# One-hot rows of the chosen keys compared for eight tokens in one instruction instead of four

## The chip, the cores and the metric

The kernel runs on one core of one Trainium2 chip. The time is the device time of one execution in microseconds (us), the median of three runs. A core has a matrix engine (TensorE, PE in the profile; PEld is its loading of weights), a vector engine (VectorE, DVE), an activation engine (ScalarE, ACT), a general engine (GpSimd, POOL) and a queue that issues transfers (SyncE, SP). Each engine runs its own instructions in the order in which they stand in the program; between engines they wait on semaphores.

## The reference, cut to what matters

The kernel computes two transformer blocks for 512 tokens of width 1024. The change lies in the expert layer of the first block. For each token, 8 heads choose 16 pairs of keys (e1, e2) out of 128 by 128, which name 128 of 16,384 experts, each with a gate; the output is a gated sum over these experts.

```
e1 = jnp.take_along_axis(i1, ic // PEER_TOPK, axis=-1)
e2 = jnp.take_along_axis(i2, ic % PEER_TOPK, axis=-1)
idx = (e1 * N_KEYS + e2).reshape(T, PEER_HEADS * PEER_TOPK)
gate = jax.nn.softmax(vc, axis=-1).reshape(T, PEER_HEADS * PEER_TOPK)
...
u = expert_u[ib]
pre = jnp.einsum('td,tkd->tk', xb, u).astype(jnp.float32)
a = jax.nn.gelu(pre, approximate=False) * gb
return jnp.einsum('tk,tkd->td', a, expert_v[ib])
```

## The kernel before

For 384 of the 512 tokens the kernel multiplies every token with every expert and weighs the products with a dense table of gates, G[e1, e2, token], which is zero where an expert was not chosen. (The last 128 tokens are done by gathering rows, later.) The table is made in what is called the gate stage here: 96 steps of four tokens each, a software pipeline of four parts, whose loop variable is `q`.

- `g_hot` (line 957): DVE compares, for four tokens, the chosen keys with a constant `iota4` (0 to 127, each value four times). The keys lie in `eT`, one chosen pair per partition, token along the free dimension. The result `eb` is of shape [128, 2, 128, 4] in bf16: for half 0 (e1) and half 1 (e2), for each of the 128 key values, for each of the four tokens, a 1 where the key was chosen. The token is the innermost run. There are two buffers of `eb`.
- `g_wide` (line 967): `eb` is read with key and token exchanged, so that a token's 128 values lie in a row. ACT copies half 1 to `o2` in float32 (line 970). For `o1`, half 0 is multiplied with the gates `gT` (line 972); that is done by GpSimd in 60 of the steps and by DVE in 36 of them. Both have three buffers.
- `g_sum` (line 975): PE makes, for each of the four tokens, the 128 by 128 product of `o2` and `o1` into `gps`. In the profile a product in float32 is two records. Behind each step it issues one or two matmuls of `early_products` (line 814, `acc<-XT,wraw`), which compute ahead some of the products of the next stage; they need neither `eb` nor `o1`.
- `g_out` (line 981): ACT copies `gps` to a staging buffer (`gst` or `rows`), which is sent to memory every eight steps from the queue of GpSimd (line 992).

Two more things run in this stage. `pair_keys` (line 911) makes the keys of the next 128 tokens, one piece every five steps: DVE compares and adds (lines 918 to 949), and one multiplication `eq<-eq,ib` of 2048 elements is done by GpSimd (line 933). And GpSimd's queue issues the transfer of each finished early product (line 824), for which it waits in its order.

The tile framework's scheduler sets the order of the instructions on each engine, from the order in which they are written and from its own estimates; behind the stage comes the loop over the experts (`prepare`, `u_product`, `v_product`), whose matmuls with line 1100 and 206 to 208 make up most of the time. `cload` (line 159) loads a constant through GpSimd's queue.

Of the kernel before, what the change touches and what calls it, by code (L numbers as in the profile page):

```python
# [12 lines left out]
BF16 = mybir.dt.bfloat16  # L13
U32 = mybir.dt.uint32
AF = mybir.ActivationFunctionType
OP = mybir.AluOpType
# [13 lines left out]
def t5_bucket(d):  # L30
    n, mx = 32, 2048
    e = n // 2
    nf = np.maximum(d, 1).astype(np.float32)
    large = e + (np.log(nf / np.float32(e)) / np.log(mx / e) * (n - e)).astype(np.int32)
    large = np.minimum(large, n - 1)
    return np.where(d < e, d, large)


def na_layout():

    def tile_(kind, n):
        r = np.repeat(np.arange(8), 16)
        if kind == "b":
            return r, n * 16 + np.tile(np.arange(16), 8)
        r8, w = np.repeat(np.arange(8), 8), np.tile(np.arange(8), 8)
        return np.concatenate([r8, r8]), np.concatenate([n * 16 + 8 + w, (n + 2) * 16 + w])

    seq = [tile_("b", 0), tile_("b", 1), tile_("m", 0), tile_("m", 1), tile_("b", 2), tile_("b", 3)]  # L50
    qr, qw = np.repeat(np.arange(8), 16), np.tile(np.arange(16), 8)
    dr = np.zeros((128, 4, 256), int)
    dc = np.zeros((128, 4, 256), int)
    ok = np.zeros((128, 4, 256), bool)
    for cb, first in enumerate(NA_FIRST):
        kr = np.concatenate([seq[first][0], seq[first + 1][0]])[None]
        kc = np.concatenate([seq[first][1], seq[first + 1][1]])[None]
        qc = cb * 16 + qw[:, None]
        lo = np.clip(qc - 8, 0, 48)
        dr[:, cb] = kr - qr[:, None] + 7  # L60
        dc[:, cb] = np.clip(kc - qc, -15, 15) + 15
        ok[:, cb] = (kc >= lo) & (kc < lo + 16)
    return dr, dc, np.where(ok, 0, NEG).astype(np.float32)


def const_arrays():
    f = np.float32
    c = {}

    sel4 = np.zeros((4, 4, 128), f)  # L70
    col4 = np.zeros((128, 4, 4), f)
    for h in range(4):
        sel4[h, h] = 1
        col4[:, h, h] = 1
    c["sel4"] = sel4
    c["col4"] = col4
    j, i = np.arange(128)[:, None], np.arange(128)[None, :]
    c["cmaskT"] = np.where(j <= i, 0, NEG).astype(f)

    d = 511 - np.arange(640)  # L80
    oh = np.zeros((32, 640), f)
    ok = d >= 0
    oh[t5_bucket(np.maximum(d, 0))[ok], np.nonzero(ok)[0]] = 1
    c["t5oh"] = oh
    cnt = (d <= 128).astype(int) + (d % 4 == 0) + (d % 16 == 0)
    cnt = np.where(ok, cnt, 0)
    ln = np.where(cnt > 0, np.log(np.maximum(cnt, 1)), NEG).astype(f)
    c["t5ln"] = np.broadcast_to(ln, (8, 640)).copy()
    c["na_mask"] = na_layout()[2]
    i, k = np.arange(128)[:, None], np.arange(384)[None]  # L90
    m = np.where(np.abs(i - (k - 128)) <= 128, 0, NEG).astype(f)
    z = np.zeros((128, 256), f)
    c["swa_mask"] = np.concatenate([z, m, z], 1)

    t = np.arange(T)
    inv = np.power(f(10000.0), -np.arange(16, dtype=f) / f(16)).astype(f)
    ang = np.concatenate([(t // 64).astype(f)[:, None] * inv, (t % 64).astype(f)[:, None] * inv], 1)
    cos, sin = np.cos(ang).astype(f), np.sin(ang).astype(f)
    tab = np.stack([np.concatenate([cos, cos], 1), np.concatenate([-sin, sin], 1)], 1)
    c["rope"] = np.ascontiguousarray(tab.reshape(4, 128, 2, 64).transpose(1, 0, 2, 3))  # L100

    c["iota4"] = np.broadcast_to(np.repeat(np.arange(128), 4).astype(f), (128, 512)).copy()
    c["rank16"] = np.broadcast_to(np.repeat(np.arange(16), 128).astype(f), (128, 2048)).copy()
    return c

# [2 lines left out]
def body(ctx: ExitStack, tc: tile.TileContext, a: dict, out: bass.AP, dbg=None, stop=None):  # L108
# [8 lines left out]
    ve, se, pe, gp, sy = nc.vector, nc.scalar, nc.tensor, nc.gpsimd, nc.sync  # L117

    def pool(stack, name, bufs=1, **kw):
        return stack.enter_context(tc.tile_pool(name=name, bufs=bufs, **kw))  # L120
# [17 lines left out]
    def t2(n=T, name="t2", p=128):  # L138
        return tp.tile([p, n], F32, name=name, tag="t2")
# [19 lines left out]
    def cload(pl, name, shape, dt=F32):  # L159
        t = pl.tile(shape, dt, name=name)  # L160
        gp.dma_start(t, a[name])
        return t
# [261 lines left out]
    with ExitStack() as mx:  # L424
# [172 lines left out]
        for hd in range(4):  # L597
# [25 lines left out]
            q = t2(T, "E")  # L623
# [145 lines left out]
    with ExitStack() as ex:  # L769
# [20 lines left out]
        eT = kp.tile([128, 2, T], BF16, name="eT")  # L790
# [43 lines left out]
        with ExitStack() as gx:  # L834
# [15 lines left out]
            for hd in range(8):  # L850
                for half in range(2):
# [7 lines left out]
                    q = t2(name="pq")  # L859
# [45 lines left out]
        with ExitStack() as gx:  # L905
            gk = pool(gx, "ghot")
            gst_ = [rows[:, :4].rearrange("p r n -> p (r n)"),
                    pool(gx, "gstage").tile([128, NE * TG], F32, name="gst")]
            iota4 = cload(gk, "iota4", [128, 512], BF16)
            i4 = iota4.rearrange("p (e t) -> p e t", t=4)  # L910
            def pair_keys(t, eng):

                tps = mix([128, 2, 128], "ktp") if t != TS else None
# [41 lines left out]


            def g_hot(it):
                tok = it["tok"]
                it["eb"] = eb = gk.tile([128, 2, 128, 4], BF16, name="eb", bufs=2)
                ve.tensor_tensor(eb, i4.unsqueeze(1).to_broadcast([128, 2, 128, 4]),  # L960
                                 eT[:, :, tok].unsqueeze(2).to_broadcast([128, 2, 128, 4]), OP.is_equal)

                t, q = divmod(it["q"], 32)
                if t < TS and q % 5 == 3:
                    next(keys[t + 1], None)
# [32 lines left out]
            for _ in keys[0]:  # L998
                ahead(10)
            pipeline([dict(q=th * (TG // 4) + tg, th=th, tg=tg, tok=slice(th * TG + tg * 4, th * TG + tg * 4 + 4))  # L1000
                      for th in range(ND // TG) for tg in range(TG // 4)], g_hot, g_wide, g_sum, g_out)
        pp.close()
        b1.close()
# [715 lines left out]
def layout(i):  # L1719
    f = np.float32  # L1720
    o = dict(const_arrays())
    o["xT"] = np.ascontiguousarray(i["x"][0].T)
    w = i["w_in"][0]
# [74 lines left out]
```

## Time and profile before

| what | us |
|---|---|
| median of three runs (range) | 3405.89 (3403.52 to 3408.29) |
| the profiled execution, its own time | 3405.12 |
| its span, first to last instruction | 3403.4 |
| PE busy | 3278.4 (96%) |
| DVE busy | 2352.6 (69%) |
| ACT busy | 1239.5 (36%) |
| POOL busy | 680.9 (20%) |
| the gate stage | about 585 to 776 of the span |

Busy time is the time in which an engine has an instruction under way, also while that instruction is held up. PE is busy nearly all the time over the whole span; the gate stage, some 191 us, is a small part of it and has limits of its own.

### The profile page before, as it was taken

What the parts mean: (1) busy time and instruction counts of PE and PEld (TensorE: products, weight loads), DVE (VectorE), ACT (ScalarE), POOL (GpSimd) and SP (SyncE); (2) the same over time, 40 slices, a digit from 0 to 9 for tenths busy, and PEclk for the clock granted to TensorE, in tenths of its full rate; (3) what the DMA queues carried; (4) which work ended last, traced back from release to release, by engine and by line L of the source; (5) the groups of instructions that cost most, each with busy time, mean ns of one, the idle gap of its engine ahead of it and who ended that gap; (6) DMA issues with size and microseconds to landing.
All of it is one profiled execution on the core that took longest, in us unless ns stands there. A gap on an engine that the chain in (4) does not pass through costs nothing.

```text
span 3403.4 us, 49823 instructions
## 1 busy us (share of the span) xinstructions
PE 3278.4 (96%) x19091; PEld 2762.9 (81%) x19091; DVE 2352.6 (69%) x4718; ACT 1239.5 (36%) x2138; POOL 680.9 (20%) x695
## 2 busy tenths in 40 slices
PE   7889999898999999999999999999999998989999
PEld 5565766677999999999989887888888887878887
DVE  5345678875777777777765557587767778757776
ACT  4134211563333333333354546321221236632221
POOL 0000011564444444444311222000000001100000
PEclk9989999999999999999999999999999999999999
DMA  4535564459888888888832212221111211023331
GB/s 155 196 116 173 176 211 145 165 194 343 296 317 310 307 300 317 305 305 312 287 114 77 72 64 72 68 83 64 67 62 62 62 39 32 14 76 117 94 99 56
DMA packets 151990, 538.07 MB, mean 158 GB/s; under 512 B 17988, under 2 KB 23332, under 8 KB 150216
## 3 DMA queue, kind: packets, MB, share of 16 engines
q1 hardware_dynamic: 97920, 326.76, 28.4%
q0 software_dynamic: 52800, 205.51, 16.9%
q8 instruction: 150, 2.46, 0.3%
q10 hardware_dynamic: 1032, 2.62, 0.2%
q14 instruction: 88, 0.72, 0.1%
HBM read 497.24 MB, written 40.13 MB: 158 GB/s over the span
## 4 chain that ended last, share of the span: by engine, by line
PE 85%; DVE 6%; DMA 3%; issue 2%; ACT 2%; POOL 1%; SPq 0%; POOLq 0%; DVEq 0%; ACTq 0%
PE pv L1100 15%; PE acc L206 11%; PE acc L207 11%; PE acc L208 11%; PE acc L232 9%; PE pd L200 3%; PE pd L199 3%; PE pd L201 3%; PE pt L347 2%; PE acc L814 2%; DMA mraw<-in_w_mod_dram 2%; PE gps L978 1%; PE mod L392 1%; PE on L1400 1%; DVE eb L960 1%
## 5 line engine op out<-in xcount | busy, mean ns | idle before, releaser
L206 PE MATMUL acc<-hh,wh 128*128 128x512 f32 (+1 forms) x1728 | 638.0, 370 | 4.9 <-DVE cg L1205 2.3
L207 PE MATMUL acc<-hl,wh 128*128 128x512 f32 (+1 forms) x1728 | 633.1, 366 | 0.0
L208 PE MATMUL acc<-hh,wl 128*128 128x512 f32 (+1 forms) x1728 | 632.2, 366 | 0.0
L206 PEld LDWEIGHTS acc<-hh,wh 128*128 128x128 f32 x1728 | 326.1, 189 | 51.4 <-issue 8.1
L207 PEld LDWEIGHTS acc<-hl,wh 128*128 128x128 f32 x1728 | 326.1, 189 | 39.4 <-issue 1.2
L208 PEld LDWEIGHTS acc<-hh,wl 128*128 128x128 f32 x1728 | 325.7, 188 | 39.3 <-issue 2.2
L183 ACT ACTIVATE wh<-wraw 128x1024 fp32r<-128x1024 f32 (+1 forms) x189 | 198.9, 1054 | 393.9 <-PE acc L207 168.0
L1100 PE MATMUL pv<-vl,ah 128*128 128x512 f32 x768 | 302.3, 394 | 10.5 <-DVE vl L1080 10.5
L1100 PE MATMUL pv<-vh,al 128*128 128x512 f32 x768 | 302.4, 394 | 0.0
L184 DVE TENSOR_TENSOR wl<-wraw,wh 128x1024 fp32r<-128x1024 f32 (+1 forms) x189 | 230.7, 1222 | 102.3 <-ACT wh L183 98.9
L1100 PE MATMUL pv<-vh,ah 128*128 128x512 f32 x768 | 298.2, 389 | 0.0
L1016 POOL DMA_INDIRECT rows<-in_expert_v_dram,sidx x128 | 191.1, 1493 | 231.5 <-DVE tok L1031 204.6
L1016 POOL DMA_INDIRECT rows<-in_expert_u_rows_dram,sidx x128 | 180.0, 1406 | 229.3 <-DVE rows L1021 217.7
L232 PE MATMUL acc<-wh,hh 128*128 128x256 f32 (+1 forms) x624 | 195.6, 314 | 3.9 <-ACT hh L183 2.3
L232 PE MATMUL acc<-wh,hl 128*128 128x256 f32 (+1 forms) x624 | 193.3, 310 | 0.0
L232 PE MATMUL acc<-wl,hh 128*128 128x256 f32 (+1 forms) x624 | 192.9, 309 | 0.0
L1074 DVE TENSOR_TENSOR al<-ge,ah 128x384 fp32r<-128x384 f32 x128 | 71.3, 557 | 171.7 <-ACT ah L1072 171.2
L1072 ACT ACTIVATE ah<-ge 128x384 fp32r<-128x384 f32 x128 | 67.3, 526 | 328.7 <-PE pv L1100 286.2
L1100 PEld LDWEIGHTS pv<-vl,ah 128*128 128x128 f32 x768 | 144.9, 189 | 39.2 <-DVE vl L1080 10.8
L1100 PEld LDWEIGHTS pv<-vh,al 128*128 128x128 f32 x768 | 145.0, 189 | 30.4
L1021 DVE SCALAR_TENSOR_TENSOR rows<-rows,tok 128x1024 f32<-128x1024 f32 x128 | 154.5, 1218 | 20.1 <-issue 17.4
L1100 PEld LDWEIGHTS pv<-vh,ah 128*128 128x128 f32 x768 | 144.5, 188 | 27.8
(460 smaller groups left out, 7349.4 us busy)
## 6 DMA issues: line engine op xcount, KB each, us to landing
wraw<-in_expert_u_dram SPq DMA_DIRECT2D x128, 512.0 KB, 5.8
vraw<-in_expert_v_dram SPq DMA_DIRECT2D x127, 512.0 KB, 4.8
mraw<-in_w_mod_dram SPq DMA_DIRECT2D x96, 512.0 KB, 4.2
wraw<-in_ffn_up_dram SPq DMA_DIRECT2D x88, 512.0 KB, 3.5
gt<-gdr POOLq DMA_DIRECT2D x31, 768.0 KB, 9.1
wraw<-in_ffn_down_dram SPq DMA_DIRECT2D x44, 512.0 KB, 4.0
gdr<-gst POOLq DMA_DIRECT2D x6, 2048.0 KB, 7.7
gdr<-rows POOLq DMA_DIRECT2D x6, 2048.0 KB, 7.6
```

Source lines behind the costliest of these rows:

```text
L183: se.activation(hi, src, AF.Copy)
L184: ve.tensor_tensor(lo, src, hi.bitcast(F32), OP.subtract)
L199: pe.matmul(ps, wh[i], xh[i], start=i == 0, stop=False)
L200: pe.matmul(ps, wh[i], xl[i], start=False, stop=False)
L201: pe.matmul(ps, wl[i], xh[i], start=False, stop=i == n - 1)
L206: pe.matmul(ps, wh[:, k], hh[:, k], start=k == 0, stop=False)
L207: pe.matmul(ps, wh[:, k], hl[:, k], start=False, stop=False)
L208: pe.matmul(ps, wl[:, k], hh[:, k], start=False, stop=k == KT - 1)
L232: pe.matmul(ps[:, i], x[:, k, s], y, start=k == 0 and i == 0 and x is hh and y is wh, stop=k == KT - 1 and i == nt - 1 and y is wl)
L1016: gp.indirect_dma_start(r, None, src, bass.IndirectOffsetOnAxis(ap=sidx[:, k:k + 1], axis=0))
L1021: pin(ve.scalar_tensor_tensor(r, r, 1.0, htok, OP.mult, OP.mult, accum_out=spre[:, k:k + 1]))
L1100: pe.matmul(sums[t][hf], x[:, s], y[:, d], start=e == 0 and y is vh and x is ah, stop=e == NE - 1 and x is al)
```

## The change

The constant `iota4` becomes `iota8`, in which each value stands eight times. `g_hot` compares in the steps of even `q` for eight tokens at once, into an `eb` of shape [128, 2, 128, 8]; the step of odd `q` takes its four tokens out of the same tile. There are still two buffers of `eb`, of twice the size. The readers in `g_wide` are unchanged in the code, but the distance between two of a token's values in `eb` is now eight bf16 values, 16 bytes, instead of four, 8 bytes.

```
-    c["iota4"] = np.broadcast_to(np.repeat(np.arange(128), 4).astype(f), (128, 512)).copy()
+    c["iota8"] = np.broadcast_to(np.repeat(np.arange(128), 8).astype(f), (128, 1024)).copy()
...
-            iota4 = cload(gk, "iota4", [128, 512], BF16)
-            i4 = iota4.rearrange("p (e t) -> p e t", t=4)
+            iota8 = cload(gk, "iota8", [128, 1024], BF16)
+            i8 = iota8.rearrange("p (e t) -> p e t", t=8)
+            ebs = {}
...
             def g_hot(it):
-                tok = it["tok"]
-                it["eb"] = eb = gk.tile([128, 2, 128, 4], BF16, name="eb", bufs=2)
-                ve.tensor_tensor(eb, i4.unsqueeze(1).to_broadcast([128, 2, 128, 4]),
-                                 eT[:, :, tok].unsqueeze(2).to_broadcast([128, 2, 128, 4]), OP.is_equal)
+
+                if it["q"] % 2 == 0:
+                    tok = slice(it["tok"].start, it["tok"].start + 8)
+                    ebs[it["q"] // 2] = eb = gk.tile([128, 2, 128, 8], BF16, name="eb", bufs=2)
+                    ve.tensor_tensor(eb, i8.unsqueeze(1).to_broadcast([128, 2, 128, 8]),
+                                     eT[:, :, tok].unsqueeze(2).to_broadcast([128, 2, 128, 8]), OP.is_equal)
+                it["eb"] = ebs[it["q"] // 2][:, :, :, it["q"] % 2 * 4:it["q"] % 2 * 4 + 4]
```

The order on DVE at the start of the gate stage, behind the copy of the first keys (`eT<-ktp`); `eb<-iota,eT` is the comparison, `o<-eb,gT` the multiplication with the gates, `eq` and `cb` belong to `pair_keys`. Before:

```order
L954 CAST eT<-ktp 128x2x128
L925 TENSOR_SCALAR cu<-ic 128x128
L960 TENSOR_TENSOR eb<-iota_4673,eT 128x1024 x2
L929 CAST cb<-cu 128x128
L927 TENSOR_SCALAR cu<-ic 128x128
L937 TENSOR_TENSOR eq<-eq 128x1024
L972 TENSOR_TENSOR o_4792<-eb,gT 128x512
L960 TENSOR_TENSOR eb<-iota_4673,eT 128x1024 x2
L972 TENSOR_TENSOR o_4821<-eb,gT 128x512
L972 TENSOR_TENSOR o_4834<-eb,gT 128x512
```

The same place of the changed kernel (its lines 960 to 976 are numbered three or four higher):

```order
L955 CAST eT<-ktp 128x2x128
L926 TENSOR_SCALAR cu<-ic 128x128
L963 TENSOR_TENSOR eb<-iota_4673,eT 128x2048 x2
L976 TENSOR_TENSOR o_4790<-eb,gT 128x512
L976 TENSOR_TENSOR o_4817<-eb,gT 128x512
L963 TENSOR_TENSOR eb<-iota_4673,eT 128x2048
L976 TENSOR_TENSOR o_4830<-eb,gT 128x512
L938 TENSOR_TENSOR eq<-eq 128x1024
```

Two comparisons of twice the size stand ahead of the first multiplications, and three small instructions of `pair_keys` have moved behind them.

The order on DVE near the end of the stage, when `pair_keys` is done. Before:

```order
L960 TENSOR_TENSOR eb<-iota_4673,eT 128x1024 x3
L972 TENSOR_TENSOR o_5877<-eb,gT 128x512
L960 TENSOR_TENSOR eb<-iota_4673,eT 128x1024 x3
L972 TENSOR_TENSOR o_5919<-eb,gT 128x512
L960 TENSOR_TENSOR eb<-iota_4673,eT 128x1024 x4
L972 TENSOR_TENSOR o_5968<-eb,gT 128x512
```

The same place of the changed kernel:

```order
L963 TENSOR_TENSOR eb<-iota_4673,eT 128x2048 x2
L976 TENSOR_TENSOR o_5805<-eb,gT 128x512
L963 TENSOR_TENSOR eb<-iota_4673,eT 128x2048 x2
L976 TENSOR_TENSOR o_5843<-eb,gT 128x512
L976 TENSOR_TENSOR o_5890<-eb,gT 128x512
L963 TENSOR_TENSOR eb<-iota_4673,eT 128x2048 x2
```

Where three comparisons stood between two multiplications, one or two of twice the size stand now.

## Rows read from the trace of the kernel before

**Rows 1.** The page: busy time of PE, and the chain that ended last.

```profile
PE 3278.4 (96%) x19091; PEld 2762.9 (81%) x19091; DVE 2352.6 (69%) x4718; ACT 1239.5 (36%) x2138; POOL 680.9 (20%) x695
...
PE pv L1100 15%; PE acc L206 11%; PE acc L207 11%; PE acc L208 11%; PE acc L232 9%; PE pd L200 3%; PE pd L199 3%; PE pd L201 3%; PE pt L347 2%; PE acc L814 2%; DMA mraw<-in_w_mod_dram 2%; PE gps L978 1%; PE mod L392 1%; PE on L1400 1%; DVE eb L960 1%
```

**Rows 2.** Windows: length; PE, PEld, DVE, ACT, POOL busy; granted clock; DMA share, GB/s.

```profile
585.00:716.00 131.00, 113.00 (x616) 88.52 (x615) 114.08 (x130) 71.48 (x128) 79.33 (x59) 0.91 0.46 166
716.00:776.00 60.00, 58.49 (x378) 48.04 (x377) 37.67 (x46) 42.65 (x77) 32.38 (x33) 1.00 0.56 205
```

**Rows 3.** Tile `eb`, all its instructions: shortest, median, longest ns.

```profile
L960 DVE TENSOR_TENSOR eb<-iota,eT x96: 676/680/4370, 588.3 to 771.4; 128x1024 bf16<-128x1024 bf16 x96
L970 ACT ACTIVATE o<-eb x96: 650/676/693, 589.1 to 773.6; 128x512 f32<-128x512 bf16 x96
L972 POOL TENSOR_TENSOR o<-eb,gT x60: 1035/1328/2582, 589.0 to 772.1; 128x512 f32<-128x512 bf16 x60
L972 DVE TENSOR_TENSOR o<-eb,gT x36: 677/679/5828, 591.2 to 772.9; 128x512 f32<-128x512 bf16 x36
```

**Rows 4.** Timeline around GpSimd's multiplication of `pair_keys` at 680.

```profile
680.16 3.84 POOL L933 TENSOR_TENSOR eq<-eq,ib 128x2048 bf16<-128x2048 bf16 x1
680.25 4.91 DVE L960 TENSOR_TENSOR eb<-iota,eT 128x1024 bf16<-128x1024 bf16 x2 [2.25 <-POOL o L972]
...
684.59 0.66 ACT L970 ACTIVATE o<-eb 128x512 f32<-128x512 bf16 x1 [5.81 <-DVE eb L960]
```

**Rows 5.** Timeline of DVE, where nothing holds it up: start, duration, count.

```profile
575.30 0.28 DVE L919 SCALAR_TENSOR_TENSOR cf<-ic,cu 128x128 f32<-128x128 uint32 x1
...
578.73 2.28 DVE L933 TENSOR_TENSOR eq<-eq,ib 128x2048 bf16<-128x2048 bf16 x1
...
583.14 1.22 DVE L931 TENSOR_TENSOR eq<-rank,cb 128x2048 bf16<-128x2048 bf16 x1
584.27 0.42 DVE L954 CAST eT<-ktp 128x256 bf16<-128x256 f32 x1
...
588.27 1.28 DVE L960 TENSOR_TENSOR eb<-iota,eT 128x1024 bf16<-128x1024 bf16 x2
```

**Rows 6.** Timeline of POOL, two multiplications back to back.

```profile
635.50 2.04 POOL L972 TENSOR_TENSOR o<-eb,gT 128x512 f32<-128x512 bf16 x2
```

**Rows 7.** Groups in 585 to 716: count, busy us, mean ns, idle before.

```profile
L960 DVE TENSOR_TENSOR eb<-iota,eT 128x1024 bf16<-128x1024 bf16 x62 | 58.6, 974 | 9.3 <-POOL o L972 5.3 <-ACT o L970 3.6
L972 DVE TENSOR_TENSOR o<-eb,gT 128x512 f32<-128x512 bf16 x24 | 21.9, 917 | 0.3 <-PE gps L978 0.2
L931 DVE TENSOR_TENSOR eq<-rank,cb 128x2048 bf16<-128x2048 bf16 x5 | 8.6, 1721 | 0.0
...
L972 POOL TENSOR_TENSOR o<-eb,gT 128x512 f32<-128x512 bf16 x36 | 47.4, 1320 | 32.2 <-DVE eb L960 22.6 <-DVE o L972 4.0 <-PE gps L978 4.0
L933 POOL TENSOR_TENSOR eq<-eq,ib 128x2048 bf16<-128x2048 bf16 x6 | 23.4, 3902 | 5.7 <-DVE eq L931 5.7
```

**Rows 8.** The same groups in 716 to 776.

```profile
L960 DVE TENSOR_TENSOR eb<-iota,eT 128x1024 bf16<-128x1024 bf16 x34 | 28.5, 867 | 20.2 <-POOL o L972 18.1 <-ACT o L970 1.7
L972 DVE TENSOR_TENSOR o<-eb,gT 128x512 f32<-128x512 bf16 x12 | 9.9, 826 | 2.0 <-PE gps L978 1.3
...
L972 POOL TENSOR_TENSOR o<-eb,gT 128x512 f32<-128x512 bf16 x24 | 27.8, 1171 | 16.1 <-DVE eb L960 11.8 <-PE gps L978 3.8 <-POOL o L972 0.5
```

**Rows 9.** Line 183, copies on ACT: shortest, median, longest ns.

```profile
L183 ACT ACTIVATE wh<-wraw x189: 443/1060/1067, 14.4 to 3344.6; 128x1024 fp32r<-128x1024 f32 x188, 128x288 fp32r<-128x288 f32 x1
...
L183 ACT ACTIVATE hh<-XT x8: 629/631/637, 378.0 to 386.2; 128x512 fp32r<-128x512 f32 x8
```

**Rows 10.** Line 1355, sums on POOL, in the same form.

```profile
L1355 POOL TENSOR_TENSOR bias<-bias,na_mask x32: 1259/1282/2241, 1752.3 to 2112.4; 128x512 f32<-128x512 f32 x32
```

**Rows 11.** The chain that ended last, behind the gate stage: start, duration.

```profile
775.56 6.47 PE acc L814 x20
...
785.57 15.19 DMA XT<-xdr
```

## The prediction

> **What bounds the kernel now.** I read the page first. PE is busy in 96% of the span and the chain that ended last is nearly all PE; of the gate stage only 1% (`gps`) and 1% (`eb`) stand in it [rows 1]. So the change can matter only as far as it moves the end of the gate stage; what follows that stage hangs on its last matmuls and on a transfer that starts behind them [rows 11], and shifts with them.
>
> Next the stage itself, by stretches. It falls into two parts. [...] From 716 to 776 PE is busy in 58.5 of 60 at clock 1.00, so PE sets the pace [rows 2].
>
> Who makes PE wait in the first part? The timeline answers. At 680.16 GpSimd starts its 3.84 us multiplication; DVE starts two comparisons at 680.25 that need 1.28 us elsewhere, and they take 4.91, until GpSimd is done and a little more; ACT then waited 5.81 us for them [rows 4, 5]. The longest comparison, 4.37, and the longest multiplication on DVE, 5.83 against 0.68 in the median, are of this kind [rows 3]. So DVE and GpSimd hardly work at the same time here; one stands until the other's instruction is done. What counts is therefore the **sum** of both engines' undisturbed work.
>
> The undisturbed prices, from start to start: a comparison 0.60 (two in 1.28, one in 0.68), one of 2048 elements 1.13 (584.27 less 583.14), a multiplication on DVE 0.60 (as long as a comparison, 0.68 each in the median), one half of `pair_keys` on DVE 3.43 (578.73 less 575.30, from behind one multiplication of `pair_keys` to the next) [rows 3, 5]. On GpSimd 1.00 for `o1` (two of them in 2.04, the shortest single one 1.035) and 3.84 for the long multiplication [rows 3, 4, 6]. With the counts of the first part: 62 x 0.60 + 24 x 0.60 + 5 x 3.43 = 68.7 on DVE, 36 x 1.00 + 6 x 3.84 = 59.0 on GpSimd, together **127.7 of 131 us, 97%** [rows 7]. In the second part: (34 + 12) x 0.60 + 24 x 1.00 = 51.6 of 60, **86%** [rows 8], and PE sets the pace.
>
> **The change part by part.**
>
> *Fewer comparisons.* 96 of 0.60 become 48 of 1.13: 0.07 each pair, 2.2 us less in the first part and 1.2 in the second. The work per element stays what it is. This is all that the change takes away by its count.
>
> *The readers' step.* A token's values lie 16 bytes apart instead of 8, for all three kinds of reader. No instruction of ACT, DVE or GpSimd that I found in this trace reads SBUF at such a step, so I bound it. Lower end for each: unchanged. Upper end for each: as though it had twice the elements, as each element now stands alone in its 16 bytes where two stood. For GpSimd that is +1.0 (two in 2.04, [rows 6]), for DVE +0.53 (0.60 to 1.13, [rows 5]), for ACT +0.38 (0.68 to the 1.06 of a copy of 1024, [rows 3, 9]). For the choice: on ACT, 512 values in a row take 0.63 and 512 at a step of 8 bytes 0.68 [rows 3, 9], a hint that the step is not quite free, no more. On GpSimd a sum of 512 whose operands lie in a row takes 1.26 at least, more than the 1.04 of `o1` [rows 3, 10], so its time goes with what it fetches and not with the elements alone. So I take half of the upper end, **+0.5, for GpSimd**, and the lower end, 0, for DVE and ACT.
>
> [...]
>
> *Sum in the first part.* 127.7 - 2.2 + 36 x 0.5 = 143.5 us of DVE and GpSimd together. Packed as tightly as now (97%) that needs 148, packed without a gap 143.5: **+12 to +17**. *In the second part:* 51.6 - 1.2 + 24 x 0.5 = 62.4. The pair of engines takes over from PE as the bound: +2.4 without a gap, +4.3 at 97%. So **+15 to +21**; gaps on PE also bring stretches of lower clock, as the 0.91 of the first part shows [rows 2], so I take the upper half, **+20**.
>
> *Start of the stage.* The first comparison is 1.13 instead of 0.60 and its readers wait for all of it: +0.5, once. It is in the rounding.
>
> *More lead.* Two buffers now hold 16 tokens instead of 8, and a comparison waits for readers that are one step older. That loosens the waits of the comparison for `o1` and ACT (5.3 and 3.6 us in the first part, 18.1 and 1.7 in the second, [rows 7, 8]). In the second part DVE waits with PE full, so nothing is gained; in the first, DVE and GpSimd together leave 131 - 127.7 = 3.3 us open. I take 0, with a bound of 3.3 + 1.5 (what PE leaves open in the second part).
>
> *The load of `iota8`.* Twice the bytes, issued ahead of the first keys and needed at 588.3 [rows 5]; the whole making of those keys, some four halves of `pair_keys` and more, covers it. 0; without that cover it would cost a transfer's time once.
>
> *The order.* The scheduler moves some pieces of `pair_keys` by a step or two on DVE, with the same work; 0, with a few us either way if one of GpSimd's long multiplications falls in front of a comparison that is waited for; each such stall costs PE some 2 to 4 us [rows 4].
>
> The sum is made against the profiled execution, 3405.1 us, which lies 0.8 under the median of the runs: 3405 + 20 = **3425**.
>
> **The rivals.**
>
> *All three readers pay.* Then 36 multiplications on DVE cost up to 0.53 more: 24 x 0.53 = 12.7 in the first part, 6.4 in the second, on the same pair of engines, some 19 to 20 us on top: about 3445 (3433 to 3455). ACT with +0.38 would be at 42.65 + 35 x 0.38 = 56 of 60 in the second part, not yet a bound [rows 2], but each step's chain grows. For it: the step is the same for all. Against it: ACT's 0.05 for the step of 8 bytes is small. [...]
>
> *No reader pays.* Then only the 2.2 us in the first part count, with the 0.5 of the start against them; the second part is PE's. About 3403.5, between 3399 and 3407: no change that can be measured. For it: on the chip's DVE and ACT here the step of 8 bytes costs nothing or 0.05. This is also the case in which the change does not do what it says: the comparisons already ran at a rate of 1024 elements in 0.60, and 2048 in 1.13 is the same rate [rows 5].
>
> *The lead pays (the other side).* If no reader pays and the doubled lead closes the gaps, the first part loses 2.2 + 3.3 and the second 1.5, and PE, waiting less, gets its clock back in part: 3396, between 3392 and 3399. The point that decides: GpSimd's `o1` must stay at about 1.05. Above 1.1 the 60 of them eat the gain.
>
> **How the numbers follow.** GpSimd pays: 0.48, with 3414 to 3433 as its own range. All pay: 0.18. None pays: 0.27. The lead pays: 0.07. The predicted time is the likeliest's, 3425. Leaving out the case of the lead, the lower end of "none pays" and the upper part of "all pay" gives 3401 to 3442. A measurement of this kernel can tell 0.2%, 7 us, from no change; so slower is 0.48 + 0.18 = 0.66, no change 0.27, faster 0.07.
>
> **What would show it.** In the changed kernel's profile: `eb` x48 at about 1.2 us undisturbed (right or wrong for the first term). POOL's `o<-eb,gT`: shortest time near 1.5 (my case), near 1.04 (none pays). DVE's `o<-eb,gT` near 0.68 or near 1.2, and ACT's near 0.68 or 1.06, tell the two slower cases apart. The stage should end near 796 instead of 776, with PE idle in its last third, which it is not now, and the span behind it should be as long as before. I am wrong in the mechanism if POOL's instruction is longer and the stage is not: then the engines overlap more than I read. I am wrong in the size if the waits pack worse than 97%.

## The result, and the profile after

The changed kernel takes **3426.15 us** (median of 5 runs, 3424.36 to 3434.26) against 3405.89 before (5 runs, 3403.52 to 3408.29): ratio 1.0064, 95% interval 1.0051 to 1.0078. It is slower, by the 20 us forecast. The profiled execution has a span of 3424.4 us. Of all executions behind this document one, of run 5, took 6308.26 us at a granted clock of 0.937 instead of 0.98; the median of run 5 counts it, the ratios leave it out.

First the readers. This is the tile `eb` of the changed kernel, all instructions on it, as in [rows 3] (shortest, median, longest ns; first and last start):

```profile
L974 ACT ACTIVATE o<-eb x96: 1106/1156/1268, 589.2 to 791.9; 128x512 f32<-128x512 bf16 x96
L976 POOL TENSOR_TENSOR o<-eb,gT x60: 1252/1512/2956, 589.1 to 790.4; 128x512 f32<-128x512 bf16 x60
L963 DVE TENSOR_TENSOR eb<-iota,eT x48: 1202/1226/4878, 587.8 to 788.0; 128x2048 bf16<-128x2048 bf16 x48
L976 DVE TENSOR_TENSOR o<-eb,gT x36: 1043/1089/6142, 590.0 to 790.8; 128x512 f32<-128x512 bf16 x36
```

All three readers got slower, by the shortest instructions: ACT 0.650 to 1.106, DVE 0.677 to 1.043, GpSimd only 1.035 to 1.252. The comparison is as forecast, 1.20 for 2048 elements.

Next the stage, in the windows of [rows 2] and the 20 us behind them (columns as there):

```profile
585.00:716.00 131.00, 101.75 (x544) 79.56 (x543) 122.41 (x95) 87.39 (x113) 85.33 (x52) 0.90 0.38 144
716.00:776.00 60.00, 55.19 (x336) 43.78 (x335) 43.26 (x27) 52.55 (x70) 40.94 (x31) 0.97 0.55 205
776.00:796.00 20.00, 19.64 (x119) 15.41 (x118) 12.21 (x9) 17.07 (x24) 11.13 (x10) 1.00 0.44 151
```

The loss is in the first part: PE is busy in 101.75 us there, 113.00 before, and shows 544 matmul records where 616 stood [rows 2]. What wasn't done there is done behind 716, where PE is busy in 55.19 of 60 and then 19.64 of 20 us. The chain that ended last shows the sum, as [rows 11] did (start, duration):

```profile
794.22 6.47 PE acc L814 x20
...
803.40 14.86 DMA XT<-xdr
```

The last block of early products starts at 794.22 instead of 775.56: 18.7 us of the 21.0 by which the spans differ. The rest lies behind it, where the change doesn't reach: from the last of these matmuls to the end pass 2621.9 us before and 2624.2 after, and between 2622.1 and 2624.5 in the traces of the runs below.

The groups of the first part in the changed kernel (as [rows 7]: count, busy us, mean ns, idle before):

```profile
L974 ACT ACTIVATE o<-eb 128x512 f32<-128x512 bf16 x54 | 61.6, 1145 | 16.6 <-DVE eb L963 16.5
L976 POOL TENSOR_TENSOR o<-eb,gT 128x512 f32<-128x512 bf16 x32 | 53.2, 1675 | 18.4 <-PE gps L982 8.7 <-issue 4.6 <-DVE eb L963 4.2
L963 DVE TENSOR_TENSOR eb<-iota,eT 128x2048 bf16<-128x2048 bf16 x29 | 52.1, 1805 | 6.0 <-POOL o L976 4.0 <-ACT o L974 1.7
L976 DVE TENSOR_TENSOR o<-eb,gT 128x512 f32<-128x512 bf16 x22 | 36.2, 1647 | 2.1 <-PE gps L982 2.1
L934 POOL TENSOR_TENSOR eq<-eq,ib 128x2048 bf16<-128x2048 bf16 x6 | 25.6, 4266 | 9.7 <-DVE eq L932 9.7
L932 DVE TENSOR_TENSOR eq<-rank,cb 128x2048 bf16<-128x2048 bf16 x5 | 8.2, 1634 | 0.1
```

GpSimd made 32 of its products here instead of 36, DVE 22 instead of 24. The mean of a DVE product is 1.65 us, though 1.04 is its undisturbed time: DVE stands while GpSimd works, as it did before [rows 4]: a product that DVE starts at 609.34, within GpSimd's multiplication from 608.37 to 613.11, takes 4.61 us.

### The profile page after: what moved, and what is told of

Its sections match the earlier page's. It is cut to its first block, busy times and chain, and to the rows that moved or that the text cites. A ratio compares the mean times of both kernels' runs of the same rounds, so it can differ in the third digit from the quotient of the medians.

```text
span 3424.4 us, 49713 instructions
## 1 busy us (share of the span) xinstructions
PE 3286.8 (96%) x19091; PEld 2768.2 (81%) x19091; DVE 2380.3 (70%) x4670; ACT 1281.4 (37%) x2138; POOL 710.9 (21%) x695
## 4 chain that ended last, share of the span: by engine, by line
PE 71%; DVE 4%; ACT 1%; issue 1%; DMA 1%; POOL 0%; SPq 0%; ACTq 0%; DVEq 0%; POOLq 0%
PE pv L1104 15%; PE acc L206 10%; PE acc L208 10%; PE acc L207 10%; PE acc L232 7%; PE pd L200 3%; PE pd L199 3%; PE pd L201 3%; PE pt L347 2%; PE on L1404 1%; PE mix L232 1%; PE s L1365 1%; PE po L206 1%; PE po L208 1%; PE po L207 1%
```

## The experiments

Twelve kernels ran, in three groups; the kernel before took 3403.85, 3404.30 and 3402.92 us in them. First the change in its two halves: the larger comparison, and the readers' step.

**1. The larger comparison alone.** One instruction for eight tokens, but the result in two blocks of four tokens, so that the readers' step stays 8 bytes (`eT` is laid out to match). The dimensions of `eb` are partition, group of four tokens, half, key and token.

```
+                    ebs[it["q"] // 2] = eb = gk.tile([128, 2, 2, 128, 4], BF16, name="eb", bufs=2)
+                    ve.tensor_tensor(eb.rearrange("p g h e t -> p (g h) e t"), i4.unsqueeze(1).to_broadcast([128, 4, 128, 4]),
+                                     eT[:, g:g + 2].rearrange("p g h t -> p (g h) t").unsqueeze(2).to_broadcast([128, 4, 128, 4]),
+                                     OP.is_equal)
+                it["eb"] = ebs[it["q"] // 2][:, it["q"] % 2]
```

> One comparison for eight tokens, as in the change, but the result lies as two blocks of four tokens, so that the readers keep their step of 8 bytes. If the readers' step is the cause: ACT near 0.68, DVE near 0.68, GpSimd near 1.04 us at the shortest, and 3399 to 3407 us. If the larger comparison itself (coarser release, other order of the instructions) is the cause: 3420 or more with the same short readers.

Measured: 3401.93, ratio 0.9998 (0.9985 to 1.0010). The readers' shortest times are as before, and there are 48 comparisons of 1.21:

```profile
L974 ACT ACTIVATE o<-eb x96: 652/676/707, 585.9 to 769.7; 128x512 f32<-128x512 bf16 x96
L976 POOL TENSOR_TENSOR o<-eb,gT x60: 1034/1057/3862, 585.8 to 768.2; 128x512 f32<-128x512 bf16 x60
L962 DVE TENSOR_TENSOR eb<-iota,eT x48: 1210/1224/5324, 584.5 to 765.4; 128x2048 bf16<-128x2048 bf16 x48
L976 DVE TENSOR_TENSOR o<-eb,gT x36: 677/689/5378, 586.8 to 769.1; 128x512 f32<-128x512 bf16 x36
```

So half as many comparisons, the lead of 16 tokens and the changed order are together worth nothing that can be measured.

**2. The step alone.** 96 comparisons of four tokens as before, written into every second group of four, 16 bytes from key to key.

```
-                it["eb"] = eb = gk.tile([128, 2, 128, 4], BF16, name="eb", bufs=2)
+                eb = gk.tile([128, 2, 128, 8], BF16, name="eb", bufs=2)
+                it["eb"] = eb = eb[:, :, :, :4]
```

> Comparisons of four tokens, 96 of them, as before, but each run of four lies 16 bytes behind the last. If the readers' step is the cause: readers as in the changed kernel (ACT 1.1 to 1.2, DVE 1.05 to 1.1, GpSimd from 1.25), and 3422 to 3434 us, the changed kernel's time and some 3 us for the 48 further comparisons. If the larger comparison is the cause: 3402 to 3410.

Measured: 3427.29, ratio 1.0074 (1.0052 to 1.0095), the whole loss. Its `eb` tile:

```profile
L961 DVE TENSOR_TENSOR eb<-iota,eT x96: 670/686/4481, 586.7 to 793.7; 128x1024 bf16<-128x1024 bf16 x96
L971 ACT ACTIVATE o<-eb x96: 1107/1147/1185, 587.5 to 795.5; 128x512 f32<-128x512 bf16 x96
L973 POOL TENSOR_TENSOR o<-eb,gT x60: 1265/1584/2887, 587.4 to 793.6; 128x512 f32<-128x512 bf16 x60
L973 DVE TENSOR_TENSOR o<-eb,gT x36: 1046/1078/1921, 589.8 to 795.6; 128x512 f32<-128x512 bf16 x36
```

The readers have the prices of the changed kernel; the comparison, which writes at this step in runs of four tokens, stays at 0.67. Runs 1 and 2 together **show** that the readers' step is the cause.

**3 and 4. The step for some of the readers.** Two comparisons for eight tokens, one for each half; in run 3 only half 0 (read by GpSimd and DVE) is at 16 bytes, in run 4 only half 1 (read by ACT). The loop shown is that of run 3; run 4 has `((0, False), (1, True))` in its place.

```
+                    for hf, wide in ((0, True), (1, False)):
...
+                            eb = gk.tile([128, 128, 8], BF16, name="eb%d" % hf, bufs=2)
...
+                            eb = gk.tile([128, 2, 128, 4], BF16, name="eb%d" % hf, bufs=2)
```

> One comparison for each half and eight tokens (96 in all, of the size before); half 0, which GpSimd and DVE read, at the step of 16 bytes, half 1, which ACT reads, at 8. If the sum of DVE and GpSimd sets the end: +0.22 on 60 and +0.39 on 36 readers, 27 us on that pair, 3420 to 3432. If ACT's 0.48 more on 96 copies is what PE waits for: 3404 to 3412.

> The other way round: half 1, which ACT reads, at the step of 16 bytes, half 0 at 8. If the sum of DVE and GpSimd sets the end: 3403 to 3411, with ACT's copies at 1.1 to 1.2. If ACT's copies are the cause: 3416 to 3428.

Measured: run 3 3421.36, ratio 1.0051 (1.0032 to 1.0070); run 4 3415.93, 1.0029 (1.0015 to 1.0043). Against 3403.85 that is +17.5 for DVE and GpSimd, and +12 for ACT alone. The second was not in my theory, and the two don't add up: 29.6 against the 20 to 23 of both together. In run 3 only GpSimd and DVE are slower (1.262 and 1.037 at the shortest, ACT 0.649), in run 4 only ACT (1.099). In run 4 DVE's and GpSimd's instructions on `eb` have their old shortest times (0.675 and 1.029), yet PE is busy in 102.73 us of the first part, as little as in run 3 (102.88). What waits there? The waits from 585 to 716 in run 4 (total, count, longest):

```profile
POOL gedr L824 <- ACT gs L820: 25.1, 7, 5.5
...
DVE eb L967 <- ACT o L983: 10.2, 7, 2.8
```

and an example from the timelines of ACT and GpSimd in run 4 (start, duration, and idle time before):

```profile
639.62 0.52 ACT L820 ACTIVATE gs<-acc 128x384 f32<-128x384 f32 x1
...
640.44 0.60 POOL L824 DMA_DIRECT2D gedr<-gs  x1 [5.55 <-ACT gs L820]
641.06 1.05 POOL L985 TENSOR_TENSOR o<-eb,gT 128x512 f32<-128x512 bf16 x1
```

GpSimd's queue stands for 5.55 us, from 634.89, in front of the transfer that stores an early product; behind the transfer GpSimd's next `o1` waits. PE has finished that product at 637.14 (the end of the last of its sixteen matmul records). The gelu of it (line 820) starts only at 639.62, because it stands on ACT behind the slower copies: 2.48 us of the wait come from there, the 2.25 ahead of them from PE. Before, these waits were 17.5 us in this part, in five places. That gave two candidates: this wait, or the buffers of the comparison, which ACT now frees later (10.2 us).

**5 and 6. The wait for the gelu taken away.** The transfer is issued behind the fifth matmul of the next early product, some four steps later, when the gelu is normally done. (The expectations say products where they mean these matmuls.) Run 5 is run 4 with this, run 6 the kernel before with it.

```
-                    gp.dma_start(gedr[SP.index(e)], t)
+                    late.append((gedr[SP.index(e)], t))
...
                 for k in range(KT):
                     m = pe.matmul(ps, raw[:, k], hf[:, k, :ND], start=k == 0, stop=k == KT - 1)
+                    if k == 4 and late:
+                        gp.dma_start(*late.pop())
```

> As the kernel in which ScalarE alone reads at a 16-byte step (3416), but each early expert's product is stored (line 824) four products later on GpSimd's queue, so that GpSimd doesn't wait for ScalarE's gelu there. If ScalarE's slower copies reach the end of the stage through that wait of GpSimd (25.1 us of waits there in the first part, 17.5 before): 3404 to 3409. If they reach it by another way (the buffers of the comparison that ScalarE frees later, ScalarE's own turn): 3413 to 3419.

> The kernel before with the later store alone, the control of the run above. If GpSimd's waits for the gelu (26.8 us in ten places) stand on the path: 3390 to 3400. If they lie beside other waits: 3402 to 3406.

Measured: run 5 3408.10, ratio 1.0007 (0.9997 to 1.0017); run 6 3401.75, 0.9995 (0.9983 to 1.0007). ACT's copies cost as much in run 5 as in run 4 (1.110 at least), and the loss of 12 us has shrunk to 4 that can't be told from none. So by these medians two thirds of ACT's part reach the end of the stage through GpSimd's place in its queue, not through ACT's own time; the intervals of the two runs overlap a little, so the share is rough. For the kernel before the move is worth nothing that can be measured. The waits for the gelu have fallen only from 41.5 in run 4 to 28.8 us in run 5 (585 to 790), so a wait's length alone does not tell what it costs.

**7. The changed kernel with the later store.**

> The changed kernel (3426) with the early experts' products stored four products later on GpSimd's queue. If part of the loss goes through GpSimd's waits for the gelu behind ScalarE's longer copies, as with ScalarE's half alone (3416 to 3408 there): 3414 to 3420. If DVE's and GpSimd's summed work alone sets the end: 3423 to 3428.

Measured: 3415.31, ratio 1.0041 (1.0027 to 1.0056), the first of the two forecasts. The changed kernel was 20.3 us above its own kernel before, this one is 12.4 above its own: about 8 of the 20 us go, with intervals that overlap a little. Its trace places most of this gain in the stage: from the first comparison (591.7) to the start of ACT's last copy of `eb` (789.4) pass 197.7 us, where the changed kernel has 204.1 (587.8 to 791.9). Since the stage began 3.9 us later in this execution, its span of 3420.0 is only 4.4 less.

**8 and 9. Is it the sum of DVE and GpSimd?** My prediction rests on the reading that the two can't work at the same time here. So their work was put on one: in run 8 every `o1` and every multiplication of `pair_keys` is DVE's; in run 9 only the latter. Step 8 bytes, as before.

```
-                (ve if it["q"] % 3 == 2 or it["q"] < 12 and it["q"] % 2 else gp).tensor_tensor(it["o1"], eb[:, 0].rearrange("p e t -> p t e"),
+                ve.tensor_tensor(it["o1"], eb[:, 0].rearrange("p e t -> p t e"),
...
-            keys = [pair_keys(t, gp if t else ve) for t in range(4)]
+            keys = [pair_keys(t, ve) for t in range(4)]
```

> The kernel before, with all 96 products of the early gates (line 972) and all multiplications of the key rows (line 933) on DVE, so that GpSimd has no tensor work in this stage. Theory A (the summed undisturbed work of DVE and GpSimd sets the first part's end): each product goes from 1.03 to 0.68 us and each multiplication gets cheaper, about 104 us of work in place of 128 in the 131 us of the first part; TensorE (113 of 131 us busy) becomes the bound there and the time falls to 3385 to 3395. Theory B (the length of the chain from one group's comparison through its readers to TensorE sets it, and two engines side by side shorten it): no gain or a loss, 3400 to 3420.

> The kernel before, with the multiplication of the key rows alone (line 933) on DVE. Theory A: about 10 us of work off the sum of DVE and GpSimd, 3394 to 3398. Theory B: DVE's queue, which the comparisons also wait in, gets 6 instructions longer: 3403 to 3410.

Measured: run 8 **3366.38**, ratio 0.9888 (0.9869 to 0.9907); run 9 3391.18, 0.9958 (0.9943 to 0.9972). Both gain more than was expected. Taking the second engine away makes the kernel faster. The windows show why; the first line is of run 9, the other two of run 8:

```profile
585.00:716.00 131.00, 115.22 (x688) 89.95 (x688) 111.76 (x143) 80.84 (x145) 64.42 (x60) 0.99 0.48 181
585.00:716.00 131.00, 130.66 (x826) 105.54 (x825) 127.58 (x213) 97.96 (x173) 11.30 (x21) 1.00 0.60 224
585.00:735.00 150.00, 149.66 (x943) 120.76 (x942) 138.20 (x230) 111.41 (x196) 12.91 (x24) 1.00 0.59 219
```

In run 8 PE is full from end to end at a granted clock of 1.00. Its comparisons and products on DVE stay at 0.70 even at their longest:

```profile
L960 DVE TENSOR_TENSOR eb<-iota,eT x96: 683/689/697, 577.1 to 726.7; 128x1024 bf16<-128x1024 bf16 x96
L970 ACT ACTIVATE o<-eb x96: 646/675/704, 577.9 to 729.1; 128x512 f32<-128x512 bf16 x96
L972 DVE TENSOR_TENSOR o<-eb,gT x96: 682/686/696, 578.3 to 728.6; 128x512 f32<-128x512 bf16 x96
```

where [rows 3] had up to 5.83 us for the same product. My expectation for run 8 was 19 us short at the least, mostly because it left the clock at 0.91: 113.00 us of PE at 0.91 and 58.49 at 1.00 [rows 2] are 161 us at full clock, so 30 of the stage's 191 could go, not 10 to 20. By the traces the stage is 33 us shorter: from the first comparison to the start of ACT's last copy of `eb` it takes 152.0 us (577.1 to 729.1), before 185.3 (588.3 to 773.6 [rows 3]). GpSimd also stands 73.6 us (585 to 760) in front of its transfers for the gelu in run 8; it has no other work there, and PE is full all the same.

**10 and 11. The change with all this work on DVE.** Run 10 is the changed kernel so, run 11 the larger comparison with the step of 8 bytes (run 1) so.

> The changed kernel with all products and key multiplications of this stage on DVE. The kernel before gained 38 us by this and TensorE became its bound (130.7 of 131 us). Here each product on DVE costs 1.07 in place of 0.69 us (96 of them: +36.5), the pairs of comparisons save 8, so DVE's 138 us of 150 become about 166, and ScalarE's 111 about 157: DVE is the bound, 3377 to 3390. If the 16-byte step costs nothing once GpSimd doesn't share with DVE: 3362 to 3368.

> One comparison for eight tokens with the readers' step left at 8 bytes, and all products and key multiplications on DVE. With TensorE as the bound the 8 us that the comparisons save lie beside it: 3362 to 3368. If the stage's end still follows DVE's work: 3356 to 3361.

Measured: run 10 3397.47, ratio 0.9986 (0.9975 to 0.9997); run 11 3370.34, 0.9908 (0.9892 to 0.9925). Run 10 is 5 us under its kernel before where run 8 is 38 under its own: with GpSimd out of the way the change costs about 32 us instead of 20 (27 against run 11, of the same group), more than the 11 to 24 expected. I had counted 12 us of DVE as free, and DVE was 97% busy already in run 8's first part (127.58 of 131). In run 10 DVE is the bound:

```profile
585.00:716.00 131.00, 113.27 (x665) 84.11 (x664) 130.97 (x146) 107.14 (x141) 9.15 (x17) 0.99 0.45 171
585.00:735.00 150.00, 132.27 (x783) 99.18 (x782) 149.58 (x167) 125.16 (x165) 10.23 (x19) 0.99 0.47 179
```

Run 11 and run 8 can't be told apart (run 11 is 2 us above the range that was expected): with PE as the bound (busy in 130.70 of the 131 us in run 11), what the larger comparisons save on DVE lies beside it (3.4 us from start to start, 48 pairs by 0.07; the 8 of the expectation added durations, which overlap). Run 8 has the lowest time of all here, 38 us under the kernel before.

**12. A step of 12 bytes**, one run: run 2 with 6 in place of 8 in the tile's shape.

> The kernel before with the four tokens of a key at a step of 12 bytes in place of 8, for the price of a reader between the two steps known. If it grows with the step: copies of ScalarE at about 0.91 us, products of DVE at 0.87, of GpSimd at 1.14. If any step over 8 bytes has the full price: 1.15, 1.07, 1.25.

Measured: 3407.08; one execution is too few to tell it from before by its time. Its readers:

```profile
L971 ACT ACTIVATE o<-eb x96: 885/913/965, 580.2 to 774.8; 128x512 f32<-128x512 bf16 x96
L973 POOL TENSOR_TENSOR o<-eb,gT x60: 1187/1492/2581, 580.1 to 773.0; 128x512 f32<-128x512 bf16 x60
L973 DVE TENSOR_TENSOR o<-eb,gT x36: 818/849/1650, 582.4 to 774.9; 128x512 f32<-128x512 bf16 x36
```

On ACT the price grows evenly with the step, 0.676, 0.913, 1.147 in the median for 8, 12 and 16 bytes (the last from run 2); on DVE the second part of the step costs more than the first, 0.679, 0.849, 1.078. GpSimd has most of its price at 12: 1.035, 1.187, 1.265 at the shortest.

The trace does tell run 12 from before. From the first comparison to the start of ACT's last copy of `eb` the stage takes 195.5 us in it and 185.3 before [rows 3]; it began 9 us earlier in this execution, which hides the difference in its time. The same length is 204.1 in the changed kernel, and in runs 1 to 4 it is 185.2, 208.8, 202.9 and 197.0, one trace each: the ones that have the wide step are longer by 12 to 24 us, as their times are.

## Why the prediction was right in size and wrong in its likeliest case

**What bounds the first part: right.** The sum of DVE and GpSimd was read from stalls in the timeline [rows 4]. Runs 8 and 9 bear it out: 60 products cheaper by 0.40 and 6 multiplications by 1.64 take 33.8 us off the sum in run 8, and its stage is 33.3 us shorter; the 6 multiplications alone take off 9.8 in run 9, and its stage is 8.0 shorter (177.3). How much of this is the sum itself and how much the clock, which rises in both, is not separated. I took the upper half of +15 to +21 on the reading that gaps on PE bring its clock down; no run shows that of gaps as such: the changed kernel's first part has 29 us without PE instead of 18, at 0.90 instead of 0.91. The prices with the wide step, from start to start, come from run 10 for DVE and from the changed kernel for GpSimd:

```profile
642.96 2.35 DVE L934 TENSOR_TENSOR eq<-eq,ib 128x2048 bf16<-128x2048 bf16 x1
645.16 1.11 DVE L976 TENSOR_TENSOR o<-eb,gT 128x512 f32<-128x512 bf16 x1
646.13 1.28 DVE L963 TENSOR_TENSOR eb<-iota,eT 128x2048 bf16<-128x2048 bf16 x1
647.26 2.11 DVE L976 TENSOR_TENSOR o<-eb,gT 128x512 f32<-128x512 bf16 x2
649.22 1.28 DVE L963 TENSOR_TENSOR eb<-iota,eT 128x2048 bf16<-128x2048 bf16 x1
...
786.67 2.52 POOL L976 TENSOR_TENSOR o<-eb,gT 128x512 f32<-128x512 bf16 x2
```

With these prices (a product on DVE 0.98, on GpSimd 1.22 to 1.27, of which I take the lower, a comparison 1.13) the changed kernel's first part holds 29 x 1.13 + 22 x 0.98 + 5 x 3.43 + 32 x 1.22 + 6 x 3.84 = 133.6 us of such work in 131. The same prices give 133.4 for run 10 (35 comparisons, 67 products, 5 halves of `pair_keys` with a multiplication of 2.20 each), where DVE alone works and is busy in 130.97. Both sums are some 2% over 131, so the prices are a little high or a little overlaps; within that both are full, against 97% before. In run 4, where ACT holds the pair up, the same count gives 122 (58 comparisons and 22 products on DVE at 0.60, 34 products on GpSimd at 1.00, the rest as in [rows 7]).

**The readers' step: the step that failed.** I took +0.5 for GpSimd and 0 for DVE and ACT, "only GpSimd pays". Measured: +0.22, +0.37 to +0.41, +0.46 to +0.48. It was the rival "all three readers pay", at a smaller price for GpSimd than either case had and a larger one for ACT than its 0.38. The total came out by luck, because the errors offset each other: on the counts of [rows 7, 8] I had added 60 x 0.5 = 30 us to the pair; the measured prices add 60 x 0.22 + 36 x 0.38 = 26.9. What led me wrong was that I looked for a hint for each engine by itself and found one for GpSimd in a sum of another type [rows 10]. The small 0.05 for the step of 8 bytes on ACT, which I put down as a hint and no more, was the better sign.

**ACT: a way that was not in the prediction.** I let ACT matter only where it would be a bound by its own time (56 of 60 us in the rival). Run 4 shows 12 us from ACT alone, and run 5 through what for the greater part: a transfer on GpSimd's queue that waits for ACT's gelu. I had named this queue in the description of the kernel and not followed it.

**The second part: wrong.** I expected DVE and GpSimd to take over as the bound and PE to have idle time there. PE is busy in 55.19 of 60 and 19.64 of the next 20, and the pair's work is about 70 of the 78 us there by the prices above (19 comparisons, 14 products on DVE, 28 on GpSimd). The second part is longer mostly because more steps are left for it. ACT makes 54 of its 96 copies of `eb` up to 716, so 42 are left, in the 78 us from 716 to the start of the last early products (794.22). Before, it had made 61, and 35 were left for 60 us [rows 11]:

```profile
L970 ACT ACTIVATE o<-eb 128x512 f32<-128x512 bf16 x61 | 40.9, 674 | 40.2 <-DVE eb L960 40.1
```

That is 1.86 us a step against 1.70: of the 19 us more, seven steps make 12.

**Fewer comparisons, the lead, the start, the order: right**, together nothing that can be measured (run 1). The rival "the lead pays" falls with it.

**What stays open.** GpSimd's and DVE's part (+17.5, run 3) and ACT's (+12, run 4) overlap, and the later store takes about 8 of the changed kernel's 20 us, though its first part is full by the sum. How much of a wait in GpSimd's queue is filled by DVE's work, and how much is lost, these runs don't separate.

## What to carry to other kernels

Before a layout is changed to save instructions, count who reads the tile and at what step: here 48 comparisons fewer saved 3 us of work on DVE, and 192 reads got longer by 0.2 to 0.5 us each. Where two engines are seen to stand for each other in the timeline, add up their work instead of looking at each one's share; moving all of it to the faster of the two can beat sharing it (run 8, -38 us). And a transfer that waits in a compute engine's queue makes that engine pay for the slowness of a third (in run 4 GpSimd stood 5.55 us in front of one store, for ACT's gelu).

## What was not expected of the hardware

- 512 bf16 values read at a step of 16 bytes take DVE 1.04 to 1.09 us and ACT 1.11 to 1.16, against 0.68 for both at 8 bytes; the writer of the same tile in runs of four values at that step (run 2's comparison) pays nothing, 0.67.
- GpSimd pays least, 1.25 against 1.035.
- Without GpSimd's tensor work beside it, the longest of 96 products on DVE is 0.696 us, against 5.83 before.
- The granted clock does not go with PE's busy time alone. In the first part it was 0.91 before, a mean over stretches at 1.00 and at 0.50 (the windows from 600 to 605 and from 590 to 595 us, for two), with PE busy in 113.00 of 131 us, but 0.99 in run 10 with 113.27, and 0.99 in run 9 with 115.22. In both of the latter GpSimd's multiplications of 3.84 us, for which DVE and ACT had stood 4.9 and 5.8 us [rows 4], are gone, but run 6, which keeps them, also has 0.95 with 113.17; what lowered the clock isn't shown. In time at full clock, 113.00 us at 0.91 are 102.8, so by this estimate the clock alone accounts for 10 of the 30 us that run 8's stage could lose.
